# Hybrid S5, attention and mixture-of-experts block: temporaries in PSUM, three more split units, a shorter warm-up and another tail

## The chip, the cores and the metric

The kernel runs on one NeuronCore of a Trainium2 chip. The metric is the device time of one execution in microseconds; of before, three runs are given, and one further execution was taken with the hardware profiler. Everything below that is a time comes from those runs or from that profile.

## The reference, cut to what matters

The input is 256 tokens of width 1024. One layer is computed, all in float32:

```
h      = rms_norm(x, ln1_g)
proj   = h @ w_in                    # 1024 -> 512 (u) + 3*512 (q,k,v) + 2*1024 (gates)
y_ssm  = s5_mixer(u, ...)            # complex diagonal scan, 32 groups, 64 states, over 256 steps
g      = gelu(y_ssm)
y_ssm  = g * sigmoid(g @ w_glu + b_glu)
y_attn = moba_attention(q, k, v)     # 8 heads of 64; 256 tokens are one block: plain causal, T5 bias
merged = sigmoid(gate_ssm) * (y_ssm @ w_up_ssm) + sigmoid(gate_attn) * (y_attn @ w_up_attn)
x      = x + merged @ w_out
h      = rms_norm(x, ln2_g)
# two-stage router: best of 4 groups, then the best 2 of its 8 experts
y      = sum over 32 experts of combine[:, e] * ((silu(h @ w1[e]) * (h @ w3[e])) @ w2[e])
out    = rms_norm(x + y, ln_f_g)
```

The experts' weights are 3 x 32 x 1024 x 512 floats, 201 MB; all other weights together are about 25 MB.

## The kernel before, in words

**Stages.** A *dense part* (norm, the input product, S5, attention, the gates, `glu`, `up`, `out`, the second norm and the router) is followed by the *expert part*: eight "quads" of four experts, for each of which up to 32 tokens per expert are gathered by a product with a one-hot matrix, multiplied with `w1`, `w3` and `w2` and scattered back. Experts with more than 32 tokens are served by a loop after the output has been written, whose count is zero for this input.

**Units.** The input product is cut into 16 units of 256 columns, in the order of the table `KN['order']`; then come `glu`, four `up` and four `out` units. A unit's 1 MB of weights is loaded into one of two raw buffers (`load_unit`, blocks 2 and 3). A *native* unit multiplies the float32 weights as they are: 16 products, which the profile records as 32. A *split* unit first writes each weight as a high part and a low part (`split`: a copy to `wh`, a subtract to `wl`, 128 x 1024 each in two halves) and then makes 48 products of the cheaper type: high x high, high x low, low x high. `KN['nat']` lists the native units, 0 to 8. The split units need the normed input in split form too (`hH`, `hL`), made at unit `KN['hs']` from `hn`. Units 0 to 2 use `h32`, the input before the factor 1/rms, and their results are scaled when they leave PSUM (`in_evac`); the others use `hn`.

**Order.** The order of all instructions is fixed when the program is built; the framework only adds the waits. S5 (`ssm_thread`), its preparation (`pool_thread`), attention and gelu are generators, of which a few steps are issued after each quarter of a unit (`bg`), by delays in the table `KN['g']`. The table `KN['e']` says which engine makes an elementwise step (A = ACT, V = DVE, G = POOL), `KN['sp']` after which quarter a split is issued.

**The stream.** The experts' weights are 192 pieces of 1 MB. `pump` issues pieces on the queue of SP into 21 SBUF slots (`KN['slots']`, block numbers in the order of their use; many of these blocks hold something else in the dense part, and a piece must wait until that is done). `KN['pump']` says how many pieces are issued before which half unit; all pieces after `out2.1` follow without anything between them. At most eight transfers of the queue are under way at a time.

**PSUM.** There are eight banks of 128 x 512 floats in two rings (`bank`): ring "a" has the results of the `in`, `glu`, `up` units and of the router, ring "b" all others; each has four banks. A bank is given out again when its last reader is done.

**Second norm and tail.** `rsqrt` is ten small DVE instructions (a bit trick and three Newton steps, L705 to L714). After the last expert the sum is scaled by 1/rms in four parts, stored by four DMAs on SP's queue (L1949), and the loop `tc.For_i` at L1957 is entered and left with a count of zero.

Of the kernel before, what the change touches and what calls it, by code (L numbers as in the profile page):

```python
# [10 lines left out]
F32 = mybir.dt.float32  # L11
# [9 lines left out]
S = 256  # L21
# [29 lines left out]
for _n, _w in (("ident", 128), ("tri", 128), ("iota1", 32), ("iota0", 32), ("rev", 32)):  # L51
# [9 lines left out]
       'D01': 'G',  # L61
# [6 lines left out]
       'M3.0': 'A',  # L68
# [67 lines left out]
       'W00.0.0': 'A',  # L136
# [3 lines left out]
       'W01.0.0': 'V',  # L140
# [6 lines left out]
       'W02.1.1': 'A',  # L147
# [25 lines left out]
       'ga2': 'V',  # L173
# [3 lines left out]
       'gb2': 'G',  # L177
# [7 lines left out]
       'ge1sh': 'G',  # L185
# [8 lines left out]
       'ge3sl': 'V',  # L194
# [6 lines left out]
       'gz1h': 'V',  # L201
# [21 lines left out]
       'out0.0.1h': 'A',  # L223
       'out0.0.1l': 'G',
# [5 lines left out]
       'out1.0.0l': 'V',  # L230
# [13 lines left out]
       'out2.1.1l': 'G',  # L244
       'out3.0.0h': 'A',
       'out3.0.0l': 'V',
       'out3.0.1h': 'V',
# [5 lines left out]
       'ra0': 'V',  # L253
# [15 lines left out]
       'up0.0.1h': 'V',  # L269
       'up0.0.1l': 'V',  # L270
       'up0.1.0h': 'A',
       'up0.1.0l': 'G',
# [10 lines left out]
       'up2.0.0h': 'A',  # L283
# [33 lines left out]
       'w13.0l': 'G',  # L317
# [44 lines left out]
       'ya1.0h': 'A',  # L362
# [26 lines left out]
       'in3.0': 3,  # L389
       'in3.1': 0,  # L390
       'in4.0': 3,
       'in4.1': 2,
# [4 lines left out]
       'in7.0': 0,  # L397
       'in7.1': 2,
       'in8.0': 1,
       'in8.1': 0,  # L400
# [6 lines left out]
       'attnmx0.128': 6,  # L407
# [15 lines left out]
       'attnsc0.128': 1,  # L423
       'attnsc0.256': 6,
# [9 lines left out]
       'attntp0.1': 1,  # L434
# [7 lines left out]
       'attnya1.1': 0,  # L442
# [6 lines left out]
       'geluge1b': 3,  # L449
# [4 lines left out]
       'geluge2b': 13,  # L454
# [18 lines left out]
       'poolP00.0': 2,  # L473
# [39 lines left out]
       'ssmT1.1.2': 0,  # L513
# [65 lines left out]
       'ssmyo3': 8},  # L579
# [20 lines left out]
       'out0.1': 2,  # L600
       'out1.0': 0,
# [5 lines left out]
       'up1.0': 1,  # L607
       'up1.1': 0,
# [3 lines left out]
       'up3.1': 0},  # L612
    'slots': [16, 18, 20, 19, 21, 10, 11, 22, 8, 15, 17, 14, 13, 9, 12, 3, 2, 4, 0, 1, 6],
    'sp': {'in1.0': 3,
       'in1.1': 0,
       'in10.0': 2,
       'in10.1': 2,
       'in11.0': 3,
       'in11.1': 2,
       'in12.0': 0,  # L620
       'in12.1': 3,
# [3 lines left out]
       'in14.1': 0,  # L625
       'in15.0': 0,
       'in15.1': 2,
       'in2.0': 3,
       'in2.1': 0,
       'in3.0': 2,  # L630
       'in3.1': 2,
# [12 lines left out]
    'nat': [0, 1, 2, 3, 4, 5, 6, 7, 8],  # L644
    'hs': 7,
    'nat2': [],
    'order': [0, 1, 2, 3, 4, 5, 6, 7, 8, 12, 9, 13, 10, 14, 11, 15],
}
# [5 lines left out]
def hybrid_block(ctx, tc, x_ch, x_tok, small, consts, bc, w_in, w_glu, w_up, w_out, rel, onehot, w_rt, w13, w2,  # L654
# [28 lines left out]
    def bank(name, tag="b"):  # L683
        return psp.tile([128, 512], F32, tag=tag, bufs=4, name=name)
# [8 lines left out]
    def pick_engine(name, default, opts):  # L693
        OPTS[name] = (default, opts)
        return engines[KN["e"].get(name, default)]
# [8 lines left out]
    def rsqrt(y, v, tmp, g):  # L704
# [60 lines left out]
    def pump(n=1):  # L765
        for _ in range(n):
# [11 lines left out]
            ready[p] = t  # L778


    sm = per.tile([128, SM_W], F32, name="sm")
# [1264 lines left out]
```

## Time and profile before

| | before |
| --- | --- |
| median of 3 runs | 677.11 us (675.61 to 679.51) |
| profiled execution | 677.7 us, of which 675.9 us are the profile's span |
| PE busy | 524.9 us, 78% of the span |
| DVE, ACT, POOL busy | 219.9, 124.8, 135.1 us |
| moved by SP's and ACT's DMAs (queue q1) | 232.51 MB |
| first expert piece issued / first expert product | 119 us / 225 us |
| last expert piece issued | 641 us |
| mean granted clock of PE | 0.87 of 2.4 GHz |

The profile divides the execution into waits (which engine stood idle until which other instruction ended), groups of equal instructions with their mean time, and a timeline. The dense part fills the first 216 us or so, the expert part the rest. A line such as L702 or L699 belongs to a helper that many steps call; what is meant is then told by the tile (`wl` is a low part, `wh` a high part, `scan` the temporaries of S5's scan, `vu` and `qk` what the first units write).

### The profile page before, as it was taken

How to read it: one execution, taken by the hardware profiler on the slowest of the kernel's cores; microseconds unless marked ns; L12 is line 12 of the kernel's file. 1: busy time of each engine (PE TensorE's matmuls, PEld its weight loads, DVE VectorE, ACT ScalarE, POOL GpSimd, SP SyncE). 2: the span in 40 equal slices, each digit the busy share in tenths (PEclk: the TensorE clock that was granted, in tenths of full speed). 3: DMA queues.
4: the chain of work that ended last, by engine and by line, in shares of the span. 5: the costliest groups of instructions: out<-in, count | busy, mean ns of one | idle time of the engine just before them, and what ended most of it. 6: DMA issues, size and time to landing. Idle time of an engine off the chain costs nothing. (4 is left out here: it accounts for less than half of the span.)

```text
span 675.9 us, 9611 instructions
## 1 busy us (share of the span) xinstructions
PE 524.9 (78%) x3931; PEld 292.3 (43%) x3931; DVE 219.9 (33%) x432; ACT 124.8 (18%) x281; POOL 135.1 (20%) x232
## 2 busy tenths in 40 slices
PE   9989999969998889696686757768766766676680
PEld 8878899859986443150041014104201400230130
DVE  5755889867785312120021011001101100120012
ACT  3362644464315010000000000001000000100021
POOL 4889455744561000000000000000000000000020
PEclk9989999998999899987689689766977976897685
DMA  7527343665899999999999999999999999999971
GB/s 264 199 87 248 125 157 126 250 250 193 324 369 423 406 422 420 421 420 422 420 421 421 421 422 421 420 422 420 422 421 421 420 420 422 420 422 421 420 317 68
DMA packets 35154, 235.02 MB, mean 348 GB/s; under 512 B 4051, under 2 KB 5244, under 8 KB 7452
## 3 DMA queue, kind: packets, MB, share of 16 engines
q1 hardware_dynamic: 34700, 232.51, 84.6%
q0 software_dynamic: 256, 1.74, 0.7%
q8 instruction: 33, 0.54, 0.3%
q14 instruction: 21, 0.17, 0.1%
q10 hardware_dynamic: 144, 0.06, 0.0%
HBM read 233.23 MB, written 2.63 MB: 349 GB/s over the span
## 5 line engine op out<-in xcount | busy, mean ns | idle before, releaser
L1856 PE MATMUL pb<-wslot,xg 128*32 128x512 f32 x512 | 87.1, 761 | 41.8 <-DMA wslot<-in_w 41.7
L1856 PE MATMUL pa<-wslot,xg 128*32 128x512 f32 x512 | 89.2, 777 | 38.2 <-DMA wslot<-in_w 38.2
L1936 POOL TENSOR_TENSOR ob<-x,xg 128x256 f32<-128x256 f32 (+1 forms) x6 | 5.3, 913 | 438.6 <-DMA wslot<-in_w 434.2
L1903 PE MATMUL py<-wslot,mt 128*32 128x256 f32 x1024 | 71.7, 421 | 24.5 <-DMA wslot<-in_w 18.9
L1889 DVE SCALAR_TENSOR_TENSOR mt<-mt,pa 128x512 f32<-128x512 f32 x8 | 5.5, 688 | 224.9 <-ACT mt L1888 224.9
L1856 PEld LDWEIGHTS pb<-wslot,xg 128*32 128x32 f32 x512 | 12.9, 120 | 114.8 <-DMA wslot<-in_w 104.9
L1903 PEld LDWEIGHTS py<-wslot,mt 128*32 128x32 f32 x1024 | 31.4, 119 | 64.6 <-DMA wslot<-in_w 31.6
L1856 PEld LDWEIGHTS pa<-wslot,xg 128*32 128x32 f32 x512 | 12.1, 120 | 100.4 <-DMA wslot<-in_w 88.1
L702 POOL TENSOR_TENSOR wl<-raw,wh 128x512 fp32r<-128x512 f32 (+1 forms) x22 | 40.3, 1836 | 33.8 <-ACT wh L699 18.5
L1919 DVE TENSOR_TENSOR x<-x,scp 128x512 f32<-128x512 f32 (+1 forms) x34 | 22.3, 657 | 58.7 <-PE scp L1918 58.7
L1839 DVE TENSOR_TENSOR xg<-xgp,sm 128x512 f32<-128x512 f32 (+1 forms) x18 | 11.4, 632 | 90.1 <-PE xgp L1837 90.1
L1918 PE MATMUL scp<-mt 128*128 128x512 f32 (+1 forms) x68 | 32.9, 609 | 7.1 <-ACT mt L1915 7.1
L1888 ACT ACTIVATE mt<-pa 128x512 f32<-128x512 f32 x8 | 4.8, 597 | 176.5 <-PE pa L1856 176.5
L1837 PEld LDWEIGHTS xgp<-mt,h 128*128 128x128 f32 x256 | 33.6, 214 | 6.3 <-issue 5.5
L1837 PE MATMUL xgp<-mt,h 128*128 128x128 f32 x256 | 35.5, 302 | 0.9 <-DVE mt L1829 0.9
L1915 ACT COPY mt<-py 128x512 f32<-128x512 f32 (+1 forms) x17 | 9.5, 561 | 125.8 <-PE py L1903 125.8
L702 DVE TENSOR_TENSOR wl<-raw,wh 128x512 fp32r<-128x512 f32 (+1 forms) x26 | 29.5, 1145 | 6.7 <-ACT wh L699 5.9
L1276 PE MATMUL inp<-hn,raw 128*128 128x256 f32 x128 | 29.8, 390 | 0.0
L1280 PE MATMUL inp<-hH,wh 128*128 128x256 f32 x112 | 28.2, 288 | 0.0
L1280 PE MATMUL inp<-hL,wh 128*128 128x256 f32 x112 | 27.6, 283 | 0.0
L1276 PEld LDWEIGHTS inp<-hn,raw 128*128 128x128 f32 x128 | 24.8, 197 | 4.0 <-DVE vu L1295 0.6
L699 ACT CAST wh<-raw 128x512 fp32r<-128x512 f32 (+1 forms) x28 | 20.7, 769 | 18.2 <-DMA raw<-in_w_out 7.9
(318 smaller groups left out, 745.6 us busy)
## 6 DMA issues: line engine op xcount, KB each, us to landing
wslot<-in_w SPq DMA_DIRECT2D x191, 1024.0 KB, 19.8
raw<-in_w_in SPq DMA_DIRECT2D x14, 1024.0 KB, 4.9
raw<-in_w_up SPq DMA_DIRECT2D x4, 1024.0 KB, 5.0
raw<-in_w_out SPq DMA_DIRECT2D x4, 1024.0 KB, 4.8
rbz<-rbd POOLq DMA_DIRECT2D x1, 1536.0 KB, 8.7
xc<-in_x_ch SPq DMA_DIRECT2D x4, 256.0 KB, 4.8
raw<-in_w_in SPq DMA_DIRECT2D x4, 256.0 KB, 5.8
raw<-in_w_in SPq DMA_DIRECT2D x2, 512.0 KB, 7.2
```

Source lines behind the costliest of these rows:

```text
L699: (A.copy if e is A else e.tensor_copy)(out_, in_)
L702: pick_engine(name, default, opts).tensor_tensor(out=out, in0=in0, in1=in1, op=op)
L1276: T.matmul(ps[:, 0:S], raws["in", u][:, k, c], (h32 if u < 3 else hn)[:, k], start=(k == 0), stop=(k == KD - 1))
L1280: T.matmul(ps[:, 0:S], (wh if x else wl)[:, k, c], (hH if y else hL)[:, k], start=first, stop=last)
L1837: T.matmul(ps[:, i * 128:i * 128 + 128], h2[:, b, k * 128:k * 128 + 128], Dt[:, b].rearrange("p e s -> p (e s)"), start=(b == 0), stop=(b ...
L1839: V.tensor_tensor(out=xg[:, ks[0]:ks[0] + n], in0=ps[:, 0:n * 128].rearrange("p (k n) -> p k n", k=n), in1=smc("g2", ks[0], ks[0] + n).uns ...
L1856: T.matmul(pab[t][32 * e:32 * e + 32], xg[:, k, 32 * e:32 * e + 32], w[:, e], start=(k == 0), stop=(k == KD - 1))
L1889: V.scalar_tensor_tensor(out=hid, in0=hid, scalar=1.0, in1=pab[0], op0=OP.add, op1=OP.mult)
L1903: T.matmul(py[32 * e:32 * e + 32, n % 2 * 256:n % 2 * 256 + 256], hidT[:, f, 32 * e:32 * e + 32], w[:, i, e], start=(f == 0), stop=(f == 3))
L1915: A.copy(ye[:, o % 512:o % 512 + m], py[:, o % 512:o % 512 + m])
L1918: T.matmul(ps[:, 0:m], DwT[:, b], ye[:, o % 512:o % 512 + m], start=True, stop=True)
L1919: V.tensor_tensor(out=x2[:, b, o:o + m], in0=x2[:, b, o:o + m], in1=ps[:, 0:m], op=OP.add)
```

## The change

1. **PSUM.** Ring "a" gets three banks, ring "b" five. Temporaries move from SBUF to PSUM: the scan of S5 works in the bank that its product wrote, and is wholly on DVE (seven of its steps were on POOL); one temporary of the products that prepare S5 (`P`, `W`), the transposed output of S5, the temporaries of gelu, `glu` and `up` follow.
2. **Split units.** Units 6, 7 and 8 are split (`nat` is 0 to 5), `hH` and `hL` are made at unit 5 instead of 7, a half of a split is now four rows of 256 columns instead of eight of 128, and unit 3 uses `h32` (`hu` is 4). `hn` lies in block 13 instead of 6, and is computed from the PSUM bank of the row factor, ahead of its copy `rstd`.
3. **Start.** 10 warm-up products instead of 24; one exponential (`vexp`) goes from DVE to POOL; one ACT instruction is issued early.
4. **1/rms.** `rsqrt` becomes a power on POOL and three DVE instructions; the first norm keeps the old one as `rsqrt_newton`.
5. **Router and first gathers.** The second half of one router product stands earlier, and the first quad's gathers are interleaved otherwise with its products.
6. **Tail.** Four scalings, two each on DVE and ACT, in order of rows; three stores on SP, one on ACT. `tc.For_i` around the overflow rounds becomes `tc.If`, with its body out of line.
7. **Tables.** Some 80 entries of engines and delays, the slots' order, and the pumps: twelve pieces are issued before `out2.1` instead of eleven.

```diff
 def bank(name, tag="b"):
-    return psp.tile([128, 512], F32, tag=tag, bufs=4, name=name)
+    return psp.tile([128, 512], F32, tag=tag, bufs=3 if tag == "a" else 5, name=name)
...
 def rsqrt(y, v, tmp, g):
+    G.tensor_tensor(out=y, in0=v, in1=mhalf, op=OP.pow)
+    V.scalar_tensor_tensor(out=g, in0=v, scalar=-0.5, in1=y, op0=OP.mult, op1=OP.mult)
+    V.tensor_tensor(out=tmp, in0=g, in1=y, op=OP.mult)
+    V.scalar_tensor_tensor(out=y, in0=tmp, scalar=1.5, in1=y, op0=OP.add, op1=OP.mult)
...
-    for i in range(24):
-        T.matmul(warm[:, 0:128], ones, ones, start=(i == 0), stop=(i == 23))
+    for i in range(10):
+        T.matmul(warm[:, 0:128], ones, ones, start=(i == 0), stop=(i == 9))
+    A.activation(out=mhalf[:, 1:2], in_=ones[:, 0:1], func=AF.Copy, scale=-0.5)
...
 def s5_scan(j, ps):
-    p2 = ps.rearrange("p (r n) -> p r n", r=2)
-    V.tensor_tensor(out=t1, in0=p2, in1=er, op=OP.mult)
-    V.tensor_tensor(out=t2, in0=p2, in1=ei, op=OP.mult)
+    ta = ps.rearrange("p (r n) -> p r n", r=2)
+    tb = t2
+    V.tensor_tensor(out=tb, in0=ta, in1=ei, op=OP.mult)
+    V.tensor_tensor(out=ta, in0=ta, in1=er, op=OP.mult)
     yield "sa%d" % j
-    tt("ga%d" % j, gg[:, 0], t1[:, 0], t2[:, 1], OP.add)
-    tt("gb%d" % j, gg[:, 1], t1[:, 1], t2[:, 0], OP.subtract)
+    V.tensor_tensor(out=ta[:, 0], in0=ta[:, 0], in1=tb[:, 1], op=OP.add)
+    V.tensor_tensor(out=ta[:, 1], in0=ta[:, 1], in1=tb[:, 0], op=OP.subtract)
...
 def norm1_rows():
-    V.tensor_copy(rstd, ps[:, 0:S])
     for i in range(2):
         c = slice(4 * i, 4 * i + 4)
-        tt("hn%d" % i, hn[:, c], h32[:, c], rstd.unsqueeze(1).to_broadcast([128, 4, S]), OP.mult)
+        V.tensor_tensor(out=hn[:, c], in0=h32[:, c], in1=ps[:, 0:S].unsqueeze(1).to_broadcast([128, 4, S]), op=OP.mult)
+    A.copy(rstd, ps[:, 0:S])
...
-    for b, o in ((0, 0), (0, 512), (1, 512), (1, 0)):
-        DS.dma_start(out[b * 128:(b + 1) * 128, o:o + 512], ob[:, b, o:o + 512])
+    for b in range(2):
+        for o in (0, 512):
...
+            (A if o and b else DS).dma_start(dst, x)
...
-    with tc.For_i(0, nc.values_load(nri[0:1, 8:9], min_val=0, max_val=1)):
+    with tc.If(nc.values_load(nri[0:1, 8:9], min_val=0, max_val=1), preferred_fallthrough_block=False):
```

What the tables do is seen in the built order. On PE, around unit 2 (raw_94) and the product `rbc` that spreads the factor 1/rms, before (inp_285 is the second half of unit 1, inp_438 the first of unit 3; a name in brackets is the engine or DMA queue that is waited for):

```order
L1276 MATMUL inp_285<-h32_78,raw_89 128x256 x8
L1276 MATMUL inp_364<-h32_78,raw_94 128x256 [waits DMAHW5_49]
L1276 MATMUL inp_364<-h32_78,raw_94 128x256 x7
L1252 MATMUL rbc_385<-sqdg_215,fs_99 128x128 [waits DVE_49] x2
L1276 MATMUL inp_417<-h32_78,raw_94 128x256 [waits PE_49]
L1276 MATMUL inp_417<-h32_78,raw_94 128x256 x7
L1276 MATMUL inp_438<-hn_79,raw_213 128x256 [waits DMAHW1_49,DVE_49]
```

and now:

```order
L1298 MATMUL inp_335<-h32_78,raw_89 128x256 x8
L1298 MATMUL inp_359<-h32_78,raw_94 128x256 [waits DMAHW5_49,PE_49]
L1298 MATMUL inp_359<-h32_78,raw_94 128x256 x7
L1272 MATMUL rbc_370<-sqdg_212,fs_99 128x128 [waits DVE_49] x2
L1298 MATMUL inp_398<-h32_78,raw_94 128x256 [waits DVE_49]
L1298 MATMUL inp_398<-h32_78,raw_94 128x256 x7
L1298 MATMUL inp_427<-h32_78,raw_210 128x256 [waits DMAHW1_49,DVE_49]
```

The second half of unit 2 takes the fourth bank of ring "a" before, and now the first bank again, so that it waits for DVE (the reader of unit 1's first half). On DVE, from the product of the row factor on, before (`vu` is the evacuation of units 0 and 1, `qk` that of unit 2, `pprep` and `W1e` belong to the preparation of S5):

```order
L1253 COPY fs<-rbc 128x256
L702 TENSOR_TENSOR hn<-h_78,fs 128x1024 x2
L1295 TENSOR_TENSOR vu<-inp,fs 128x256 x4
L702 TENSOR_TENSOR scan<-s5a,fs 128x256 x4
L702 TENSOR_TENSOR s5a<-scan 128x256 x2
L1297 TENSOR_TENSOR qk<-inp,fs 128x256
L699 COPY W1e<-s5a 64x4x16
```

and now:

```order
L1275 TENSOR_TENSOR hn<-h_78,rbc 128x1024 x2
L1317 TENSOR_TENSOR vu<-inp,fs 128x256 x4
L709 TENSOR_TENSOR scan<-s5a,fs 128x256 x4
L709 TENSOR_TENSOR s5a<-scan 128x256 x2
L706 COPY Uy<-vu 32x4x64 x3
L1321 TENSOR_TENSOR qk<-inp,fs 128x256
L1029 TENSOR_TENSOR ppp<-s5a,fs 128x256
L1030 TENSOR_TENSOR pprep<-s5a,fs 128x256
L1010 TENSOR_TENSOR ppp<-ppp,pprep 128x256
```

The evacuations `vu` stand behind both halves of `hn` in either, without the copy ahead of them now; two products `P` of the preparation of S5 stood ahead of this piece and stand behind it. Further on, the first scan of S5 on DVE now (`wh` and `wl` ahead of it are those of unit 6, `hL` the low part of the normed input):

```order
L1563 TENSOR_TENSOR hL<-hn,hH 128x1024
L706 CAST wh<-raw 128x1024
L709 TENSOR_TENSOR wl<-raw,wh 128x1024
L1563 TENSOR_TENSOR hL<-hn,hH 128x1024
L706 CAST wh<-raw 128x1024
L709 TENSOR_TENSOR wl<-raw,wh 128x1024
L1109 TENSOR_TENSOR scan<-stp,E 128x512
L1110 TENSOR_TENSOR stp<-stp,E 128x512
L1112 TENSOR_TENSOR stp<-stp,scan 128x256
```

Before, the six rows ahead of the scan were not there: `hL` stood behind it, and unit 6 had no split.

## Rows read from the trace of the kernel before

**Rows 1.** The page: busy us (share of the span) x instructions of each engine.
```profile
PE 524.9 (78%) x3931; PEld 292.3 (43%) x3931; DVE 219.9 (33%) x432; ACT 124.8 (18%) x281; POOL 135.1 (20%) x232
```
**Rows 2.** Waits of SP's queue: us in total, times, longest us.
```profile
SPq L774 <- DMA wslot<-in_w: 333.0, 158, 3.1
SPq L774 <- PE pa L1856: 20.4, 7, 13.0
```
**Rows 3.** Stretches: us, busy (x instructions) of each engine, granted clock, DMA share, GB/s.
```profile
44.60:47.50 2.90, 2.82 (x8) 2.38 (x9) 1.85 (x3) 1.31 (x6) 2.64 (x5) 0.50 0.03 8
100.00:120.00 20.00, 19.22 (x178) 18.95 (x180) 19.66 (x25) 9.68 (x16) 11.34 (x6) 1.00 0.36 112
...
225.00:230.00 5.00, 5.00 (x42) 1.90 (x41) 0.85 (x2) 0.00 (x0) 0.00 (x0) 0.99 0.96 362
230.00:650.00 420.00, 302.95 (x2298) 99.30 (x2294) 48.20 (x90) 22.80 (x43) 0.00 (x0) 0.83 1.01 421
```
**Rows 4.** Timeline of PE in the first 48 us: start, duration, instruction, idle before.
```profile
1.06 8.30 PE L828 MATMUL warm<-fs 128*128 128x128 f32 x48 [1.06 <-DVE fs L825]
9.19 7.07 PE L1528 MATMUL inp<-h,raw 128*128 128x256 f32 x32
...
26.46 0.61 PE L1252 MATMUL rbc<-sqdg,fs 128*128 128x128 f32 x4
26.91 3.62 PE L1276 MATMUL inp<-h,raw 128*128 128x256 f32 x16
...
44.68 0.90 PE L1053 MATMUL m1p<-co,W1e 128*128 128x128 f32 x3 [2.39 <-ACT W1e L699]
```
**Rows 5.** Timeline of DVE: the first `h`, then `hn` and `vu`.
```profile
7.31 0.61 DVE L1525 TENSOR_SCALAR h<-xc,sm 128x256 f32<-128x256 f32 x2
27.57 2.46 DVE L702 TENSOR_TENSOR hn<-h,fs 128x1024 f32<-128x1024 f32 x2
29.95 1.40 DVE L1295 TENSOR_TENSOR vu<-inp,fs 128x256 f32<-128x256 f32 x4
```
**Rows 6.** Two stretches of PE: products of a split unit, then of native units.
```profile
111.50:117.20 5.70, 5.70 (x49) 1.00 0.55 184
31.20:41.80 10.60, 10.60 (x49) 1.00 0.50 170
```
**Rows 7.** Groups of equal DVE instructions, 89 to 145 us: busy us, mean ns.
```profile
L702 DVE TENSOR_TENSOR wl<-raw,wh 128x1024 fp32r<-128x1024 f32 x7 | 11.2, 1607 | 0.4 <-PE inp L1276 0.4
L992 DVE TENSOR_TENSOR Pe<-pprep 64x256 f32<-64x256 f32 x4 | 5.9, 1465 | 0.1
L1097 DVE TENSOR_TENSOR_SCAN scan<-E,scan 128x256 f32<-128x256 f32 x4 | 4.7, 1217 | 0.0
...
L1011 DVE TENSOR_TENSOR pprep<-s5a,fs 128x256 f32<-128x256 f32 x2 | 0.8, 421 | 0.0
...
L1089 DVE TENSOR_TENSOR scan<-stp,E 128x512 f32<-128x512 f32 x2 | 1.4, 688 | 0.1
```
**Rows 8.** Waits of PE: us in total, times, longest us.
```profile
PE glp L1454 <- DVE gHL L699: 2.6, 1, 2.6
...
PE inp L1280 <- POOL wl L702: 0.8, 1, 0.8
```
**Rows 9.** Timeline of POOL and DVE, 100 to 106 us.
```profile
100.73 4.94 POOL L702 TENSOR_TENSOR wl<-raw,wh 128x1024 fp32r<-128x1024 f32 x2 [2.87 <-ACT wh L699]
100.92 5.04 DVE L992 TENSOR_TENSOR Pe<-pprep 64x256 f32<-64x256 f32 x2
```
**Rows 10.** The tail: 1/rms (first and last row), the stores, SP's branches (ns min/median/max).
```profile
661.78 0.17 DVE L705 TENSOR_SCALAR mt<-mt 128x2 int32<-128x2 int32 x1
663.43 0.16 DVE L710 SCALAR_TENSOR_TENSOR mt<-mt 128x2 f32<-128x2 f32 x1
664.41 3.59 SPq L1949 DMA_DIRECT2D out_dram<-ob  x4
L1957 SPq COMPARE_BRANCH  x3: 38/46/54, 669.3 to 674.9; - x3
```

More of the change, by code (lines that the diff above doesn't have):

```diff
@@ L214 @@
        'hb3': 'G',
+       'ke5.1': 'V',
+       'm0h': 'V',
        'm1l': 'V',
@@ L243 @@
        'out2.1.1h': 'V',
-       'out2.1.1l': 'G',
+       'out2.1.1l': 'V',
        'out3.0.0h': 'A',
        'out3.0.0l': 'V',
-       'out3.0.1h': 'V',
+       'out3.0.1h': 'G',
        'out3.0.1l': 'G',
@@ L252 @@
        'out3.1.1l': 'V',
-       'ra0': 'V',
+       'qe0': 'A',
+       'qe1': 'V',
+       'qe5.1': 'V',
+       'ra0': 'G',
        'ra1': 'V',
@@ L396 @@
        'in6.1': 0,
[L397 to L398 removed]
+       'in7.0': 2,
+       'in7.1': 3,
        'in8.0': 1,
[L400 removed]
+       'in8.1': 2,
        'in9.0': 0,
@@ L611 @@
        'up3.0': 1,
-       'up3.1': 0},
-    'slots': [16, 18, 20, 19, 21, 10, 11, 22, 8, 15, 17, 14, 13, 9, 12, 3, 2, 4, 0, 1, 6],
-    'sp': {'in1.0': 3,
+       'up3.1': 1},
+    'slots': [18, 16, 20, 19, 21, 8, 11, 22, 15, 13, 9, 12, 10, 3, 2, 14, 6, 4, 0, 1, 17],
+    'sp': {'in1.0': 1,
        'in1.1': 0,
        'in10.0': 2,
[L617 to L621, printed above, removed]
+       'in10.1': 0,
+       'in11.0': 0,
+       'in11.1': 0,
+       'in12.0': 1,
+       'in12.1': 2,
        'in13.0': 0,
@@ L694, in pick_engine @@
         OPTS[name] = (default, opts)
-        return engines[KN["e"].get(name, default)]
+        e = KN["e"].get(name, default)
+        return engines[e if e in opts else default]
     def copy(name, out_, in_, default="A", opts="AV"):
@@ L778, in pump @@
             ready[p] = t
-    sm = per.tile([128, SM_W], F32, name="sm")
+    sm = per.tile([128, SM_W + 2], F32, name="sm")
     co = per.tile([128, CO_W], F32, name="co")
@@ L791, in hybrid_block @@
     h32 = carve(blk(7, "h32"), (KD, S))[0]
-    hn = carve(blk(6, "hn"), (KD, S))[0]
+    hn = carve(blk(13, "hn"), (KD, S))[0]
     native = set(("in", u) for u in KN["nat"]) | set(KN["nat2"])
-    A.dma_start(sm, small)
+    A.dma_start(sm[:, 0:SM_W], small)
     for k in range(0, KD, 2):
@@ L1010, in prep_P @@
                 p1, p2 = (pp1, pp2) if ri else (pp3, pp4)
+                if E is V:
+                    p1 = carve(bank("ppp"), (4, L, 16))[0]
                 E.tensor_tensor(out=p1, in0=x1, in1=y1, op=OP.mult)
@@ L1039, in prep_W @@
         E = pick_engine("W%d.%d" % (j, ri), "V", "GV")
-        p1, p2 = wq1, wq2
+        p1, p2 = (carve(bank("wpp"), (4, L - 1, 16))[0] if E is V else wq1), wq2
         E.tensor_tensor(out=p1, in0=x1, in1=y1, op=OP.mult)
@@ L1243, in norm1 @@
         V.tensor_scalar(out=v1, in0=ss1, scalar1=1.0 / DM, scalar2=EPS, op0=OP.mult, op1=OP.add)
-        rsqrt(rtk, v1, t1, g1)
+        rsqrt_newton(rtk, v1, t1, g1)
         for b in range(2):
@@ L1268, in in_split @@
         raw = raws["in", u]
-        c = slice(part * 128, part * 128 + 128)
-        split("w%d.%d" % (u, part), raw[:, :, c], wh[:, :, c], wl[:, :, c])
+        c = slice(part * 4, part * 4 + 4)
+        name = "w%d.%d" % (u, part)
+        copy(name + "h", wh[:, c], raw[:, c], opts="AV")
+        tt(name + "l", wl[:, c], raw[:, c], wh[:, c].bitcast(F32), OP.subtract)
     def in_mm(ps, u, b, part):
@@ L1409, in gelu_thread @@
         yield from until("attn")
-        gel, ge1 = carve(blk(8, "gel"), (4, S), (4, S))
+        gel = carve(blk(8, "gel"), (4, S))[0]
+        ge1 = []
+        for i in range(2):
+            ge1 += carve(bank("ge"), (S,), (S,))
         if "glu" in native:
@@ L1479, in hybrid_block @@
     units = [("in", u) for u in KN["order"]]
+    assert KN["hs"] >= 3 and all(u in KN["nat"] for u in range(KN["hu"]))
+    assert all(u in KN["nat"] or KN["order"].index(u) > KN["order"].index(KN["hs"]) for u in range(16))
     units.insert(KN["glu"], ("glu", 0))
@@ L1730, in hybrid_block @@
     x2_add(3)
-    logits(0, range(4))
+    logits(0, range(8))
     x2_tp(3, A.copy)
@@ L1735, in hybrid_block @@
     rsqrt(rs2, v2, rw1, rw2)
-    logits(0, range(4, 8))
     logits(1, range(8))
```

254 lines of the change are left out of this document (129 added, 125 removed).

## The prediction

> **What bounds the kernel now.** The page comes first, and it misleads: PE is busy for 78% of the span [rows 1], but its two halves have different limits. In the windows, the stretch from 230 to 650 us moves 421 GB/s with the DMAs' share at 1.0 while PE has idle time and DVE 48 us of work in 420 [rows 3]; in the waits of SP's queue, 333 us go by in waiting for earlier pieces, in 158 waits of at most 3.1 us [rows 2]. So the experts' part is a stream of 1 MB pieces, one per 1.049 MB / 421 GB/s = 2.49 us. Nothing that this change does to PE, DVE or POOL counts in there. The end is set by three things: when the stream is full, how full it stays at the turn to the experts, and the tail. At the turn the 21 slots are full: SP waits 20.4 us in all, once 13.0 us, for the first expert products to free one [rows 2], and from 225 to 230 us only 362 GB/s are moved [rows 3], a loss of 5 x (1 - 362/421) = 0.7 us. Hence stream and products are about level there, and an earlier dense part pays in full only if pieces and products both move up.
>
> In the dense part the timeline of PE shows hardly a gap; where it shows one, the clock adds to it. Before 44.68 us PE waited 2.39 us for ACT's `W1e` [rows 4], and in the 2.9 us behind it the granted clock was 0.50 of 2.4 GHz [rows 3], which is 1.2 GHz, so that wait cost 2.39 + 1.45 = 3.8 us. From 100 to 120 us DVE is busy for 19.66 of 20 us [rows 3]: there DVE is as much a bound as PE (19.22), and PE's longest waits later in the dense part are DVE's (2.6 us for `gHL`) [rows 8].
>
> **The start.** Warm-up takes 8.30 us for 48 records, to 9.36 us, and the first real product starts at 9.19 [rows 4]. Ten products instead of 24 end near 1.06 + 8.30 x 10/24 = 4.5 us. The first `h` is made on DVE at 7.31 us [rows 5], behind the chain of small instructions that goes to POOL, so the first product can come up to 1.9 us sooner. Against it: PE is then idle for about 3 us, a little more than the 2.39 us behind which it ran at 1.2 GHz; the same price again is 1.45 us. I take -0.4, with -1.9 and +1.5 as the ends.
>
> **The new bank wait.** With three banks in ring "a" the second half of unit 2, which started at 26.91 us [rows 4], takes the bank of unit 1's first half, and waits until DVE has read that. On DVE the two halves of `hn` (2.46 us) stand ahead of the four `vu` (1.40 us), of which the third is wanted [rows 5]. `rbc` ends at 27.1; 27.1 + 2.46 + 3/4 x 1.40 = 30.6 us. PE stands 3.7 us, and as it was the longer wait, the clock's 1.45 us come on top. In return everything behind it, ACT's `W1e` apart, is later by as much, so that the old wait of 3.8 us (its clock included) closes: PE now gets to the product that needs `W1e` at 44.7 + 2 us or so. Behind the waiting instruction on PE stand only the rest of unit 2 and unit 3, which nobody but `qk` waits for. Sum +1.3 us; the ends are -0.5 (no clock loss) and +5.2 (the old wait stays, because two products `P` now stand between `hn` and `W1e` on DVE).
>
> **Three more split units.** 49 split products take 5.70 us, and 49 records of native products take 10.60 [rows 6]. A unit has 48 of the former, 5.6 us, or 32 of the latter, 6.9 us: 1.3 us less for each, 4.0 us for three. The splitting is elsewhere: six halves on ACT, DVE and POOL. The wait for POOL's `wl`, 0.8 us [rows 8], goes too: that `wl` was to be written where `hn` lay, and had to wait for the last native unit; `hn` is now in another block. So PE's own path through the dense part changes by -0.4 + 1.3 - 4.0 - 0.8 = -3.9 us.
>
> **DVE.** In the full stretch DVE gets six steps of POOL's with 256 columns and one with 512: by 0.421 and 0.688 us that is 6 x 0.42 + 0.69 = 3.2 us; and three halves `wl` of units 11 and 13, by the mean of 1.607 us another 4.8 [rows 7]. In return DVE loses what POOL costs it. `Pe` took 5.04 us for two while POOL made two `wl` from 100.73 to 105.67 us [rows 9], and 1.465 us in the mean, where an instruction with as many columns takes 0.421; the scans took 1.217, at most 0.69 of which are their own, by an instruction of twice their columns [rows 7]. That is 4 x 1.04 + 4 x 0.53 = 6.3 us. The step with one operand in PSUM (`scan<-stp`) kept its 0.688 us [rows 7]. The change puts one operand of just these steps into PSUM. If all of the 6.3 us goes, DVE is at 8.0 - 6.3 = +1.7 us; if the `wl`, with less work on POOL beside them, also come down, below that; if nothing goes, +8.0. Where the two engines hand over to one another I expect neither PE's -3.9 nor DVE's +1.7 alone: DVE had slack before 89 us and the wait of 2.6 us is at the end only. I take -2.5 us for the whole dense part, nearer to PE since it has the longer dense stretches; the ends are -6.7 and +8.
>
> The Trainium skill, "SBUF — State Buffer", section "Who interferes with whom", says that a DVE instruction with two SBUF inputs excludes a GpSimd instruction that reads SBUF for its whole length, and that one with at most one SBUF input does not meet it. The trace agrees at the rows just named. By that rule all of the relief is certain, and the `wl`, which keep two SBUF inputs, keep their price; its result is the first rival below.
>
> **Turn to the experts.** `rsqrt` was ten instructions from 661.78 to 663.6 in the tail [rows 10], 1.8 us, and the same ten stand in the second norm. Now there are three, 3 x 0.19, and a power on POOL with two handovers. No power is in the trace; bounds are 0 and the longest POOL group here, 2.5 us for a `wl` half [rows 9]; I take 0.7, nearer to small operands. So the first product moves up 0.5 us, and the first gathers interleaved otherwise another 1 us. Of this only the dip of 0.7 us can be won. The pumps: one more piece ahead of `out2.1` is worth up to 2.49 us if it goes into idle DMA time; two slots that come free later than their place in the list lose as much. I take 0, with 2.5 us either way.
>
> **The tail.** 1/rms: -0.5 us, from above. Four stores take 3.59 us on SP [rows 10]; three of them there and one on ACT save a quarter, -0.9. SP's three branch comparisons lie between 669.3 and 674.9 us [rows 10], and all of this is behind the last store and for a count of zero. With `tc.If` and the body out of line one comparison stays ahead of the end, so up to 5.6 us could go, but the stores still have to land: I take -2.6, about half. The tail is -4.0; the ends are -1.0 (every barrier stays) and -6.
>
> **The sum** is made against the profiled execution, 677.7 us (span 675.9): -2.5 dense part, -0.7 dip, 0 pumps, -4.0 tail = -7.2, so 670.5; the median of the runs is 0.6 us below that execution, and I say 670.3 us.
>
> **The rivals.**
> (a) *DVE is fully relieved.* POOL and DVE no longer meet, DVE drops off PE's path, and the 2.6 us of `gHL` go as well: dense part -3.9 - 2.6 = -6.5, dip -0.7, tail -5: 665.5 us. For it: the rows with PSUM operands. Against: the `wl` halves on DVE, seven in this stretch before [rows 7] and more now, can still lie beside POOL's.
> (b) *DVE eats PE's gain.* Split units finish sooner and PE waits for scans and gelu instead: dense part 0, the rest as forecast: 673 us. For it: 19.66 of 20 us busy.
> (c) *The branch keeps its barriers.* Tail -1.0 to -1.5: 673 us.
> (d) *Slower: DVE's list is too long.* The six rows of unit 6's split and `hL` stand ahead of the first scan, and `wl` of units 11 and 13 ahead of gelu; if nothing of the 6.3 us comes back because the remaining `wl` are stretched in its place, the gelu chain, on which `glu` and `up` wait, is 8.0 us later: 677.7 + 8 - 4 = 681.7 us. It decides from the point where gelu's first step, not unit 15, ends the dense part, about 4 us of added DVE work. For it: DVE's full slices; against: the six steps of 256 columns are short, and DVE waited for POOL's answer at each of them.
>
> **How the numbers follow.** Forecast 0.50 (its own range 666.5 to 673.7), (a) 0.14, (b) 0.15, (c) 0.09, (d) 0.12. Faster and slower mean by over 0.5% of 677.1, about the smallest change that three runs can tell: below 673.7 or above 680.5. Faster: 0.47 of the forecast, 0.14 of (a), half of (b) and of (c): 0.73. Slower: two thirds of (d), 0.08. The rest, 0.19, is no change. The range of 664.5 to 677 leaves out (d) and the lower part of (a).
>
> **What would show it.** PE's timeline: an idle time of 3 to 4 us ending near 30 us on DVE's `vu`, and no wait for `W1e`. The groups: `Pe` and the scans near their undisturbed times, the `wl` at 1.6 us or above. The start of the first expert product at 220 to 222 us. In the tail, one comparison on SP, and 4 us less from the last product to the end. I am wrong if the wait for `gHL` grows beyond 5 us (rivals b, d), if DMA throughput between 200 and 230 us dips by more than before (the slots), or if SP's comparisons stay three.

## The result and the profile after

The changed kernel is slower: 686.0 us (median of 4 runs, 685.46 to 688.11) against 677.3 us (4 runs), a ratio of 1.0132 with a 95% interval of 1.0096 to 1.0169. That is outside the forecast range of 664.5 to 677. The profiled execution took 688.1 us, the slowest of the four; its span is 686.0 us, 10.1 us longer than that of before, and the losses below add up to those 10.1 us.

To see where the time went, take the start of the same stage in both timelines (us; the last two columns are two of the experiments below):

| stage | before | after | difference | rbz late | four put right, loop |
| --- | --- | --- | --- | --- | --- |
| first product | 9.19 | 5.64 | -3.55 | 5.49 | 5.48 |
| `rbc` (row factor) | 26.46 | 23.78 | -2.68 | 23.19 | 23.55 |
| `rbp`, after unit 2 | 30.45 | 36.63 | +6.18 | 35.84 | 29.39 |
| first S5 product `stp` | 54.72 | 56.48 | +1.77 | 55.69 | 49.78 |
| first K product `kp`, units 6 to 8 | 75.15 | 84.24 | +9.09 | 76.09 | 70.91 |
| first `glu` product | 149.15 | 158.40 | +9.25 | 151.57 | 144.15 |
| first `up` product | 165.31 | 173.39 | +8.09 | 166.16 | 160.21 |
| first expert product | 225.27 | 231.66 | +6.40 | 224.95 | 217.38 |
| last piece issued | 640.56 | 650.27 | +9.71 | 643.61 | 634.50 |
| end of the span | 675.92 | 686.02 | +10.09 | 678.90 | 669.06 |

Five things are to be read from the third column: a fast start that is thrown away by 36 us and nearly made good by 56 us, 7 us lost between 56 and 84 us, 2.9 us won between `glu` and the first expert product, 3.3 us lost from there to the last piece, and a tail that gives nothing back. Every start comes from a single profiled execution, and those lie up to 8 us from the median of their version; where a time and a start disagree below, the time, which comes from several executions, weighs more.

**The start.** The timeline of PE after (start, duration, instruction, idle before it), which answers to [rows 4]:

```profile
1.06 4.64 PE L843 MATMUL warm<-fs 128*128 128x128 f32 x20 [1.06 <-DVE fs L838]
5.64 7.94 PE L1554 MATMUL inp<-h,raw 128*128 128x256 f32 x32
...
23.78 0.61 PE L1272 MATMUL rbc<-sqdg,fs 128*128 128x128 f32 x4
31.46 5.24 PE L1298 MATMUL inp<-h,raw 128*128 128x256 f32 x16 [7.08 <-DVE vu L1317]
...
47.83 0.60 PE L1071 MATMUL m1p<-co,W1e 128*128 128x128 f32 x4
```

The warm-up ends at 5.70 us and the products follow at once, at 5.64 (ends on PE are modelled); there is no idle time between. The new wait for the bank is 7.08 us, not 3.7, and the half unit behind it takes 5.24 us instead of 3.62. DVE in that stretch:

```profile
25.27 0.18 DVE L948 TENSOR_TENSOR fs<-sm 128x16 f32<-128x16 f32 x1 [3.87 <-POOL fs L917]
...
27.48 2.34 DVE L1275 TENSOR_TENSOR hn<-h,rbc 128x1024 f32<-128x1024 f32 x2
30.32 1.42 DVE L1317 TENSOR_TENSOR vu<-inp,fs 128x256 f32<-128x256 f32 x4 [0.49 <-ACT fs L1276]
```

DVE stood 3.87 us for the last of POOL's small instructions, because the exponential had been put ahead of them on POOL; a chain of thirteen instructions that starts from that result stands ahead of `hn` and `vu` on DVE. At 47.83 us there is no wait for `W1e` any more.

**Units 6 to 8.** The weights of unit 6 are asked for behind the 1.5 MB copy `rbz` now. The issues, first before (SP's queue, then POOL; the copy comes 0.7 us later):

```profile
50.15 0.33 SPq L739 DMA_DIRECT2D raw<-in_w_in  x1
...
50.85 0.57 POOL L1320 DMA_DIRECT2D rbz<-rbd  x1 [1.45 <-DMA rbd<-t]
```

and after (POOL, then SP's queue; the copy comes 1.95 us sooner than the weights):

```profile
49.97 0.57 POOL L1342 DMA_DIRECT2D rbz<-rbd  x1 [2.23 <-DMA rbd<-t]
...
51.92 9.85 SPq L752 DMA_DIRECT2D raw<-in_w_in  x2
```

Unit 6's weights took 5.0 us to land before and 10.7 after. DVE, PE and POOL, in this order, show what came of it:

```profile
62.64 1.01 DVE L706 CAST wh<-raw 128x1024 fp32r<-128x1024 f32 x1 [6.50 <-DMA raw<-in_w_in]
63.69 1.53 DVE L709 TENSOR_TENSOR wl<-raw,wh 128x1024 fp32r<-128x1024 f32 x1
...
77.46 3.30 DVE L709 TENSOR_TENSOR wl<-raw,wh 128x1024 fp32r<-128x1024 f32 x1
```
```profile
63.80 0.36 PE L1312 MATMUL inp<-wh,hH 128*128 128x256 f32 x1 [1.95 <-DVE wh L706]
...
77.48 0.39 PE L1312 MATMUL inp<-wh,hH 128*128 128x256 f32 x1 [1.56 <-DVE wh L706]
...
80.81 1.22 PE L1312 MATMUL inp<-wl,hH 128*128 128x256 f32 x8 [1.15 <-DVE wl L709]
```
```profile
74.49 5.19 POOL L709 TENSOR_TENSOR wl<-raw,wh 128x1024 fp32r<-128x1024 f32 x2 [2.57 <-DMA raw<-in_w_in]
```

DVE had nothing to do for 6.5 us, and then the split of unit 6, `hL`, the first scan and the split of unit 7 all at once; one `wl` took 3.30 us beside POOL's. PE waited three times here, 4.7 us in all, and after the first of these waits it ran at 1.2 GHz; it did so again after a later wait of 2.0 us for `wh` at 102.1 us (granted clock 0.50 and 0.51, the column behind the busy times of PE, PEld, DVE, ACT and POOL):

```profile
65.30:72.10 6.80, 6.80 (x31) 5.76 (x31) 6.56 (x8) 0.00 (x0) 6.46 (x7) 0.50 0.46 146
102.80:106.20 3.40, 3.40 (x19) 3.40 (x18) 3.33 (x6) 0.80 (x2) 3.32 (x4) 0.51 0.44 120
```

6.80 us at half speed are worth 3.4 us. With the waits that is 8.1 us, where the stage lost 7.3: the shorter products had won less than 1 us by then.

**DVE relieved.** The groups that answer to [rows 7], 98 to 155 us of the changed kernel:

```profile
L709 DVE TENSOR_TENSOR wl<-raw,wh 128x1024 fp32r<-128x1024 f32 x10 | 13.7, 1365 | 2.2 <-ACT wh L706 2.0
L1117 DVE TENSOR_TENSOR_SCAN stp<-E,stp 128x256 f32<-128x256 f32 x4 | 2.8, 695 | 0.1
...
L1008 DVE TENSOR_TENSOR Pe<-ppp,pprep 64x256 f32<-64x256 f32 x4 | 1.7, 422 | 0.1
```

The steps with an operand in PSUM have their undisturbed times: 0.695 us instead of 1.217, 0.422 instead of 1.465. That fits a dense part that loses nothing more behind 84 us; no run here takes the PSUM operands alone out of the change.

**The tail.** From the last DVE or ACT scaling to the end before took 10.7 us and after 11.8. The power, the stores on two queues, and SP's last branch:

```profile
671.52 0.72 POOL L712 TENSOR_TENSOR mt<-mt,sm 128x2 f32<-128x2 f32 x1
...
673.58 2.63 SPq L1976 DMA_DIRECT2D out_dram<-ob  x3
674.27 0.36 ACTq L1976 DMA_DIRECT2D out_dram<-ob  x1
```
```profile
L1984 SPq COMPARE_BRANCH  x2: 41/47/53, 677.2 to 679.5; - x2
```
```profile
L2069 SPq EVENT_SEMAPHORE  x5: 28/28/28, 682.6 to 682.9; - x5
...
L2069 SPq EVENT_SEMAPHORE  x7: 17/28/28, 684.8 to 686.0; - x7
```

There are still two comparisons; behind the second SP stands for 3.1 us, and once more, between two semaphores of one list, for 1.9 us, while no other engine has work left.

### The profile page after: what moved, and what is told of

Read it like the earlier page. It is cut to its first block, busy times and chain, and to the rows that moved or that the text cites. A ratio compares the mean times of both kernels' runs of the same rounds, so it can differ in the third digit from the quotient of the medians.

```text
span 686.0 us, 9624 instructions
## 1 busy us (share of the span) xinstructions
PE 529.4 (77%) x3951; PEld 291.6 (43%) x3951; DVE 218.8 (32%) x436; ACT 123.0 (18%) x275; POOL 132.8 (19%) x253
## 5 line engine op out<-in xcount | busy, mean ns | idle before, releaser
L1882 PE MATMUL pb<-wslot,xg 128*32 128x512 f32 x512 | 91.8, 799 | 40.2 <-DMA wslot<-in_w 40.2
L1930 PE MATMUL py<-wslot,mt 128*32 128x256 f32 x1024 | 75.4, 440 | 21.4 <-DMA wslot<-in_w 15.7
L709 POOL TENSOR_TENSOR wl<-raw,wh 128x512 fp32r<-128x512 f32 (+1 forms) x21 | 37.6, 1795 | 41.9 <-ACT wh L706 26.2
L709 DVE TENSOR_TENSOR wl<-raw,wh 128x512 fp32r<-128x512 f32 (+1 forms) x33 | 41.0, 1254 | 12.7 <-ACT wh L706 10.5
L1865 DVE TENSOR_TENSOR xg<-xgp,sm 128x512 f32<-128x512 f32 (+2 forms) x19 | 11.5, 608 | 90.0 <-PE xgp L1863 90.0
L1302 PE MATMUL inp<-hH,wh 128*128 128x256 f32 x128 | 32.7, 292 | 2.0 <-DVE wh L706 2.0
L1863 PEld LDWEIGHTS xgp<-mt,h 128*128 128x128 f32 x256 | 31.1, 201 | 6.7 <-issue 6.7
L1302 PE MATMUL inp<-hL,wh 128*128 128x256 f32 x128 | 31.9, 285 | 0.0
L1298 PE MATMUL inp<-h,raw 128*128 128x256 f32 x96 | 22.9, 400 | 7.1 <-DVE vu L1317 7.1
L1302 PEld LDWEIGHTS inp<-hH,wh 128*128 128x128 f32 x128 | 24.8, 194 | 2.7 <-DVE wh L706 2.2
## 6 DMA issues: line engine op xcount, KB each, us to landing
rbz<-rbd POOLq DMA_DIRECT2D x1, 1536.0 KB, 10.7
```

The lines of the kernel that those rows point to most:

```text
L709: pick_engine(name, default, opts).tensor_tensor(out=out, in0=in0, in1=in1, op=op)
L1298: T.matmul(ps[:, 0:S], raws["in", u][:, k, c], (h32 if u < KN["hu"] else hn)[:, k], start=(k == 0), stop=(k == KD - 1))
L1302: T.matmul(ps[:, 0:S], (wh if x else wl)[:, k, c], (hH if y else hL)[:, k], start=first, stop=last)
L1863: T.matmul(ps[:, i * 128:i * 128 + 128], h2[:, b, k * 128:k * 128 + 128], Dt[:, b].rearrange("p e s -> p (e s)"), start=(b == 0), stop=(b ...
L1865: V.tensor_tensor(out=xg[:, ks[0]:ks[0] + n], in0=ps[:, 0:n * 128].rearrange("p (k n) -> p k n", k=n), in1=smc("g2", ks[0], ks[0] + n).uns ...
L1882: T.matmul(pab[t][32 * e:32 * e + 32], xg[:, k, 32 * e:32 * e + 32], w[:, e], start=(k == 0), stop=(k == KD - 1))
```

## The experiments

The main theory after the result: unit 6's weights land late because `rbz` goes first, and the split units, which need them sooner than native ones, pass that on (called "late splits" or "landing"). Rivals: the lost start itself, DVE's list, the slot order.

**Native units again.**
```diff
-    'nat': [0, 1, 2, 3, 4, 5],
-    'hs': 5,
+    'nat': [0, 1, 2, 3, 4, 5, 6, 7, 8],
+    'hs': 7,
...
-    hn = carve(blk(13, "hn"), (KD, S))[0]
+    hn = carve(blk(6, "hn"), (KD, S))[0]
```


> The changed kernel with units 6, 7 and 8 native again (hH and hL made at unit 7, hn in block 6 as before); all else as changed. Theory 'late splits' (the split units 6 to 8 come too late: their weights land late and stand in a long list on DVE, and PE then runs at half clock): the 7 us that the dense part loses between the first S5 product at 56.5 us and the K products at 84.2 us are gone, the glu products start at 151 to 152 us instead of 158.4, and the time is about 679 us. Rival 'start' (the 7.1 us wait of PE for a bank in unit 2 is what is never made good): glu still starts at 157 us or later, time 685 to 686 us. Rival 'stream' (the slot order alone): dense part 1 us shorter at most, 685 us.

679.3 us, ratio 1.0038 (1.0017 to 1.0058) to before; `glu` at 151.29 us. The weights land as late (62.26 us), but PE itself waits only 1.2 us for them:

```profile
62.40 1.10 PE L1308 MATMUL inp<-raw,hn 128*128 128x256 f32 x4 [1.17 <-DMA raw<-in_w_in]
```

So 6.7 of the 8.7 us are gone without the three split units, although the wait for the bank stays (6.4 us here): the start costs that much only where split units follow it.

**The exponential on DVE.**
```diff
-       'vexp': 'G',
+       'vexp': 'V',
```


> The changed kernel with the exponential back on DVE: POOL's chain of small instructions ends about 4 us sooner and DVE no longer waits for it ahead of hn. All theories: unit 2's second half starts at about 27.5 us instead of 31.5. Theory 'late splits': some of this reaches unit 6 (its weights are asked for when unit 4 is done), but DVE's list and the landing still bind there; glu at 155 us, time 683 us. Rival 'start': the whole 4 us and the clock's share go through, glu at 152 to 153 us, time 680 us. Rival 'stream': 686 us.

680.5 us (676.7 to 682.8), 1.0041 (1.0019 to 1.0064). The wait for the bank is 4.0 us instead of 7.1, `glu` is at 153.19: close to the rival 'start' (152 to 153 us, 680 us). The copy still goes first (47.02 against 49.11 us) and the weights still take 10.3 us to land, but all is 2.8 us sooner and PE's clock falls for half as long in units 6 to 8. So 5.5 us come back with the order of the two DMAs unchanged.

**`rbz` behind unit 6's weights.**
```diff
         raws[key] = t
+        if key == ("in", 6):                # in load_unit, behind the load
+            DS.dma_start(rbz, ...)
...
         G.dma_start(rbd, rbs)
-        G.dma_start(rbz, ...)
```


> The changed kernel with the 1.5 MB copy of the attention bias (rbz) issued on SP's queue behind the load of unit 6's weights, instead of 2 us ahead of it on POOL's. Nothing is left out. Theory 'late splits', with the landing as its cause: the weights land at 57 us instead of 62.6, PE no longer waits 1.95 us for wh at 63.8 us and its clock does not fall there; glu at 154 us, time 682 us. Rival (DVE's list is the cause, not the landing): units 7 and 8 still wait for wh and wl, glu at 157 us or later, time 685 to 686 us. Rival 'start': no change.

680.0 us, 1.0044 (1.0027 to 1.0062); `kp` starts at 76.09 us instead of 84.24 and `glu` at 151.57. The split now begins 5.4 us sooner:

```profile
57.20 0.69 DVE L706 CAST wh<-raw 128x1024 fp32r<-128x1024 f32 x1 [2.68 <-DMA raw<-in_w_in]
```

With nothing changed but the order of two DMAs and the queue of the copy, 6.0 us come back, 2 us more than the theory had expected: in the changed kernel the landing, which is down from 10.7 to 6.0 us, is the cause of most of what the split units lose.

**Slots.**
```diff
-    'slots': [18, 16, 20, 19, 21, 8, 11, 22, 15, 13, 9, 12, 10, 3, 2, 14, 6, 4, 0, 1, 17],
+    'slots': [16, 18, 20, 19, 21, 10, 11, 22, 8, 15, 17, 14, 13, 9, 12, 3, 2, 4, 0, 1, 6],
...
-    n_w = [0]
+    n_w = [1]
```


> The changed kernel with the slot order of before, and the split buffers of all units swapped, so that the last out unit uses the same blocks as before. The dense part and the first expert product (231.7 us) stay within 1 us. Theory 'stream' (3 of the 10 us are lost at the turn to the experts, because two slots that come free late, blocks 2 and 3, stand earlier in the list and blocks 4 and 6 now come free one unit later): the 21st piece is issued at about 219 us instead of 223, the last piece 3 us sooner, time 683 us. Rival (the stream only follows the first expert product): 686 us.

684.6 us, 1.0111 (1.0072 to 1.0149). In the profile the last piece is issued 418.6 us after the first expert product in the changed kernel, 417.2 here and 415.3 before: 1.4 of the 3.3 us. The 21st piece is issued at 220.5 us, later than expected. The direction agrees; 1.4 us between medians is less than these runs can tell from chance.

A rival that no run tests is PE's clock at the turn. In the first 4.4 us from the first expert product on, first before, then in the changed kernel:

```profile
225.30:229.70 4.40, 4.40 (x41) 1.77 (x40) 0.85 (x2) 0.00 (x0) 0.00 (x0) 1.00 0.96 357
```
```profile
231.60:236.00 4.40, 4.40 (x20) 1.36 (x20) 0.29 (x1) 0.00 (x0) 0.00 (x0) 0.51 0.98 411
```

Before, the clock is back at 2.4 GHz when the experts start; after, it stays at 1.2 GHz for another 4.3 us, and PE gets half as many products done. With the old slots it stays there for 2.9 us. Over all fourteen profiled executions this time ranges from 0 to 4.3 us, and the time from the first expert product to the last piece rises with it from 415.2 to 418.7 us (correlation 0.93), with the old slots as with the new ones. By the fitted line, 0.64 us for each us, the clock would make 2.6 of the 3.3 us, an estimate from a correlation and not from an edit; a share of the slots is not shown.

**Split units in the kernel before.**
```diff
-    'nat': [0, 1, 2, 3, 4, 5, 6, 7, 8],
-    'hs': 7,
+    'nat': [0, 1, 2, 3, 4, 5],
+    'hs': 5,
...
-    n_w = [0]
+    n_w = [1]
...
-    hn = carve(blk(6, "hn"), (KD, S))[0]
+    hn = carve(blk(13, "hn"), (KD, S))[0]
```


> The kernel before with units 6, 7 and 8 split (hH and hL at unit 5, hn in block 13, the two pairs of split buffers swapped so that the out units use the blocks of before); nothing else of the change. Theory 'landing' (the split units lose only where the bias copy rbz goes ahead of unit 6's weights; here the weights are asked for 0.7 us ahead of it): up's first product within 2 us of before (165.3 us) and time 675 to 679 us. Rival 'DVE list' (the six rows of unit 6's split ahead of the first scan, and scans and wl that stretch beside POOL, make the S5 chain late whatever the landing): up's first product at 169 us or later, time 681 us or more.

684.8 us, 1.0095 (1.0062 to 1.0128), `up` at 178.9 us in the profiled run: the rival's side. But the condition of the expectation did not hold: the weights were asked for at 51.53 us, behind `rbz` at 50.70, and landed at 61.5. So it does not tell the two apart. The profiled execution took 692.65 us, 7.9 us above the median of the six, so its starts overstate the loss.

**The same with `rbz` behind unit 6's weights.**


> The kernel before with units 6, 7 and 8 split, and rbz issued on SP's queue behind unit 6's weights. Theory 'landing': the weights land at 56 to 57 us instead of 61.5, PE's wait of 6.3 us and the clock's loss behind it go, up's first product at 167 to 170 us instead of 178.9, time 678 to 680 us. Rival 'DVE list' (scan and split on DVE, stretched beside POOL, bind whatever the landing): up at 174 us or later, time 683 us or more.

682.4 us, 1.0091 (1.0055 to 1.0126). The weights land at 55.1 us and `kp` starts at 74.76 us, 0.4 us sooner than before instead of 10.5 later. But `up` is at 169.99, because of a new wait (us in total, times, longest us):

```profile
PE yp L1119 <- DVE Thp L699: 7.7, 2, 7.3
```

By the starts, the landing made 8.9 of the 13.6 us and DVE's list 4.7; but the 13.6 are from the long execution. By the times the two versions are only 2.4 us apart, with nearly the same interval, and 5.0 us of the loss against the kernel before stay with the weights in time. So in the kernel before most of the loss is the rival's, and what the landing costs there is not settled. In the changed kernel with `rbz` late, `up` is 0.9 us late only; there the scans work in PSUM, which fits, but much else differs too.

**Four banks.**
```diff
-    bufs=3 if tag == "a" else 5
+    bufs=4
```


> The changed kernel with four banks in each ring; the exponential stays on POOL. Unit 2's second half no longer waits for vu: it starts at 24.2 us instead of 31.5. Theory: unit 3's first half then waits for the same vu (its bank), so 3.6 us of the 7.1 us go and the rest moves there; unit 6's weights are asked for at 48 to 49 us, but so is less of the clock lost; glu at 153 to 155 us, time 682 us. Rival 'start' (the bank wait is the loss): glu at 151 us or sooner, time 679 us or less. Rival 'ring b too small': new waits for banks in the S5 stage, time 688 us or more.

677.5 us, 0.9993 (0.9972 to 1.0014), `glu` at 148.45 us: more than I expected, on the side of the rival 'start'. But here the order of the two DMAs changes as well: unit 4 is done sooner, and the weights now go ahead of the copy (SP, then POOL):

```profile
47.80 0.33 SPq L752 DMA_DIRECT2D raw<-in_w_in  x1
...
49.14 0.57 POOL L1342 DMA_DIRECT2D rbz<-rbd  x1 [1.47 <-DMA rbd<-t]
```

They land 6.3 us after the issue. With `rbz` late and the bank wait still there `up` starts at 166.16 us, here at 164.17, in the changed kernel at 173.39. From these three starts I estimate that the bank wait costs 2 us by its length, and some 7 by what it pushes behind the copy.

**`tc.If` alone, in the kernel before.**
```diff
-    with tc.For_i(0, nc.values_load(nri[0:1, 8:9], ...)):
+    with tc.If(nc.values_load(nri[0:1, 8:9], ...), preferred_fallthrough_block=False):
```


> The kernel before with tc.If, body out of line, in place of the tc.For_i around the overflow rounds; nothing else. From the trace of the changed kernel: one jump of about 3 us over the body stays, and the queue's semaphores that stood ahead of it stand behind it. Theory 'no gain': from the last DVE scaling to the end as long as before within 0.7 us, time 677 us. Rival (the If saves what the prediction said and the stores on two queues lost it): 2 to 3 us less, 674.5 us.

680.0 us, 1.0032 (1.0008 to 1.0056): slower, which neither expectation had. From the last scaling to the end it takes 11.95 us, 10.74 before. SP's semaphores behind the jump, first before, in one go and 3 us behind the comparison at 671.3, then with the If, with a second stop between 675.3 and 677.1:

```profile
L1957 SPq EVENT_SEMAPHORE  x10: 28/28/28, 674.2 to 674.8; - x10
```
```profile
L2042 SPq EVENT_SEMAPHORE  x4: 28/28/28, 675.0 to 675.3; - x4
...
L2042 SPq EVENT_SEMAPHORE  x8: 17/28/28, 677.1 to 678.3; - x8
```

The other 1.1 us of the profiled difference arise in the dense part, which the edit doesn't touch, between 136 and 145 us.

**Four things put right at once**: the exponential on DVE, `rbz` late, slots and split buffers of before, and `rstd` and the evacuations `vu` ahead of `hn`:
```diff
+        A.copy(rstd, ps[:, 0:S])
+        flush()                          # vu, ahead of hn
         for i in range(2):
             ...                          # hn
-        A.copy(rstd, ps[:, 0:S])
```


> The changed kernel with four things put right: the exponential on DVE, rbz issued behind unit 6's weights, the slot order and split buffers of before, and on DVE the evacuations vu ahead of hn. Nothing is left out. If the three causes (POOL chain and bank wait, landing of unit 6's weights, slots) add up: unit 2's second half at 26 us, first expert product at 219 to 221 us, the 21st piece issued at 211 to 213 us, time 671 to 674 us, below both kernels. Rival (DVE's list binds the middle of the dense part whatever comes ahead): first expert product at 224 to 226 us, time 676 to 679 us.

671.0 us, 0.9886 (0.9856 to 0.9917): faster than both kernels, as expected if the causes add up. Unit 2's second half starts at 25.74 us after a wait of 1.58:

```profile
25.74 3.72 PE L1301 MATMUL inp<-h,raw 128*128 128x256 f32 x16 [1.58 <-DVE vu L1320]
```

**... and with the loop instead of `tc.If`.**


> The version with four things put right, and the loop tc.For_i of before around the overflow rounds in place of tc.If. From the run with tc.If alone in the kernel before (tail 1.2 us longer, a second stop of 1.8 us among SP's last semaphores): 1 to 2 us less than with tc.If, 669 to 670 us. Rival (the If cost nothing, the difference there was chance): 671 us.

668.7 us, 0.9869 (0.9845 to 0.9894), the lowest median of all. One stop of 3.2 us is left on SP, and 10.3 us from the last scaling to the end (12.6 with the If).

**... and with native units 6 to 8**, with the If, then with the loop:


> The version with four things put right, but with units 6, 7 and 8 native (hH and hL at unit 7, hn in block 6, split buffers as before). Theory 'landing' (with its weights in time a split unit pays): first expert product 2 to 4 us later than with the split units (220.8 us), time 673 to 675 us. Rival (the split units only move the waiting to DVE and pay nothing; with late rbz alone and with native units alone, up began at the same time): within 1 us, 671 us.

> The version with four things put right, units 6, 7 and 8 native, and the loop tc.For_i of before. From the two runs with one of these each: the loop takes off 1.2 to 2.3 us, so 670 to 671 us with up's first product at 158.7 us; the version with split units and the loop took 668.7 us, with up at 160.2. Theory (the dense part is no longer what sets the end, the stream is): no gain over that version in spite of the 1.5 us in the dense part. Rival (the dense part pays in full): 667 us.

672.5 us, 0.9926 (0.9898 to 0.9954), and 670.2 us, 0.9883 (0.9865 to 0.9901). `up` starts at 158.7 and 159.0 us, 1.2 to 3.5 us sooner than with the split units (160.2 and 162.2), and the time is 1.6 us longer in either pair, with intervals that overlap. The profiled execution of the version with split units and the If took 675.53 us, 4.6 above its median, so the 3.5 us are not to be trusted. Starts and times point in opposite ways, by less than these runs can tell from chance: whether the split units pay with their weights in time is not settled, and neither expectation is confirmed for `tc.If`; with the loop the time is the one that the theory expected.

In each of the five profiled executions with the loop SP stops once behind the branch over the body; in each of the nine with the If it stops twice, and the last stretch takes 11.3 to 12.6 us instead of 9.9 to 10.7.

## Why the prediction was wrong

**The step that failed is "Three more split units"**, put at -4.0 us with "the splitting is elsewhere". From the first S5 product to `kp` the dense part lost 7.3 us instead: 4.7 us of waits for split weights and 3.4 us of slower clock, less what the shorter products won. The step priced only PE. It took the weights as there, while a split needs them an ACT or DVE pass before the first product, and it did not look at the margin by which they were asked for ahead of `rbz`, 0.7 us. The runs put 6.0 us on the order of those two DMAs and 6.7 us on the split units as a whole; these are not two terms of a sum, since each edit takes away much of the same loss.

**"The new bank wait"** was seen, with its cause, and mis-sized: 7.1 us for 3.7. The prediction took DVE as free when `rbc` ends; POOL's longer chain, the price of moving the exponential, stood ahead of `hn`. With the exponential back on DVE the wait was 4.0 us. With four banks and all else as changed the kernel lost nothing against before (677.5 us), so this wait stands first in the chain that ends with the late weights. By the first S5 product the net was +1.8 us, where start and bank wait had been put at +0.9; that they are so near is luck, since the start was misjudged by 2.3 us the other way. That the wait for `W1e` would close was right. (The lower end of the term, -0.5, does not follow from its parts: 3.7 - 3.8 is -0.1.) What I missed is that even a small delay there decides which DMA goes first.

**"The start"** was better than forecast: -2.7 us at `rbc`, for -0.4. PE was not idle behind the shorter warm-up. The step had kept the first `h` at 7.31 us although the instructions ahead of it on DVE go to POOL, and it came at 5.06; and the ten warm-up products took 4.64 us, more than 10/24 of the old 8.30:

```profile
5.06 0.35 DVE L1551 TENSOR_SCALAR h<-xc,sm 128x256 f32<-128x256 f32 x1 [0.31 <-DMA sm<-in_small]
```

**"DVE"** was right in its mechanism: the relief came, in the instructions named and nearly to the figure; 4 x (1.465 - 0.422) + 4 x (1.217 - 0.695) is 6.3 us. The steps with one operand in PSUM were undisturbed, and `wl`, with two in SBUF, was still stretched, to 3.30 us in one case; in the mean it took 1.365 us, where 1.6 or more had been forecast. That agrees with the rule that the prediction cites from the Trainium skill ("SBUF — State Buffer", "Who interferes with whom"). The wait for `gHL`, by whose growth (b) and (d) were to be known, was 2.7 us after 2.6. Rival (d) had the right sign and a time 4.3 us too low, but for the wrong place: not gelu's chain but unit 6 was late.

**"Turn to the experts":** from the first `up` to the first expert product 1.7 us were won, where 1.5 had been forecast for second norm and gathers. That is in part luck: from the router's product (`lgp`) to that of the first gather (`xgp`) 1.1 us were won, from there to the first expert product 1.7, and 1.1 were lost ahead of them. "Pumps", put at 0, lost 3.3 us in the profile. No term of the sum had PE's clock at the turn, with which this loss goes; the slot order, which goes with 1.4 us of it in one run, is not shown to have a share.

**"The tail"**, put at -4.0, gave +0.4. 1/rms and the scalings took 0.6 us less; the stores were issued 2.2 us sooner after the scaling, but the end waits for their landing, which came 4.7 us after the scaling instead of 5.5; and the If, which was to save 2.6 us, costs 1.2 us alone.

## What to carry to other kernels

Before a load gets a consumer that needs it sooner, look at what else is issued within a microsecond of it on any queue: in the changed kernel the order of two transfers, which 0.7 us had decided before, was worth 6 us, and an edit far ahead of them (the fourth bank) turned that order round. A step that moves to another engine can be late by that engine's whole list, and what stands behind it on the next engine inherits that: here DVE stood for 3.9 us. Price a shorter product with the work of the engines that prepare it: here three split units were to save PE 4 us, and no run shows a gain of the kernel that is clear of chance.

## What the hardware showed that I had not expected

A load of 1 MB issued 2 us behind a 1.5 MB copy landed after 10.7 us, and after 6.0 us when issued 0.4 us ahead of it; in the five profiled executions with the copy first, on POOL's queue, it was 10.0 to 11.0 us. Behind the branch over the body of a `tc.If` out of line SP stood for 3.1 us, as behind the loop's (2.9 us), and then a second time, 1.7 to 2.0 us, in the straight code that follows; why is not shown. A power on POOL of 128 x 2 elements took 0.72 us.
